# Down projection: the copying and adding transfers of the plain blocks in another order

## The chip, the cores and the metric

The kernel runs on one core of one Trainium2 chip. The metric is device time in microseconds (us), the median of three runs. A separate profiled execution gives the trace from which durations are read.

## What is computed

One decoder layer on 512 tokens of width 1024. Two token mixers and a first layer norm come first; the part that matters here is the end, a gated feed-forward net, a residual and a second layer norm:

```
ff = (silu(h @ w_ff_gate) * (h @ w_ff_up)) @ w_ff_down
x  = layer_norm(DN_ALPHA * h + ff, ln2_g, ln2_b)
```

`w_ff_down` has 2816 rows, that is 22 blocks of 128, and 1024 columns.

## The kernel before

Every matrix product is made of three fp32r products: each operand is rounded to a "hi" part, the remainder is a "lo" part, and hi·hi, hi·lo and lo·hi are summed in PSUM. So each weight tile needs two steps before TensorE (PE) can use it: a rounding to hi, and a subtraction that gives lo.

The down projection treats the first 16 row blocks by a seven-product scheme (products 1 to 7 of sums and differences of quarter matrices, instead of eight). The last 6 row blocks are **plain**: six tiles of 128 x 1024, three for the left half of the columns (`("a", 0..2)`) and three for the right half (`("b", 0..2)`). They are used directly.

`dn_jobs` (L1568) is the order in which PE uses weight tiles: four tiles of product 1, four of 2, four of 5, three plain b, four of 6, four of 3, four of 7, three plain a, four of 4. A tile of a numbered product takes 12 matmuls of 512 columns (`use`, L1676), a plain one 24 (`use_plain`, L1707). The tiles live in five **slots** (`whi0` to `whi4` with `wlo0` to `wlo4`). When PE has used a tile, `release_dn` (L1683) hands its slot to the next entry of `dn_prep` (L1569 to L1572). So entry number n of `dn_prep` starts when use number n-5 is over, and a moved entry starts sooner or later by as many uses as it was moved.

How a tile is prepared depends on its kind (`prepare_dn`, L1588):

- A numbered tile: VectorE (DVE) forms the sum or difference in place where the product needs one, ScalarE (ACT) rounds it (`act.copy`, in `two_steps`, L1583), and DVE subtracts. The subtraction is held back and sent when the next `two_steps` is called (`w.flush`).
- A plain tile does not pass through DVE. GpSimd (POOL) issues a transfer from HBM that rounds on the way into `whi` (L1594; the **rounding** transfer, 512 KB). `plain_lo` then lets ACT write -hi into `wlo` (L1577, "negation" below), and POOL issues a second transfer of the same data that adds to it (L1578; the **adding** transfer), which leaves the remainder. The negation must wait for the rounding transfer to land, the adding transfer for the negation, and PE for the adding transfer.

All engines work strictly in the order in which the program lists their instructions. POOL's twelve transfers thus form one list: a rounding transfer that stands behind an adding transfer is not issued before that one, even if its slot is free.

`events` (L1736) says what else happens behind a given use: pieces of the activations being split (`piece`, `split_plain`), accumulators being added into the residual (`take`), further loads on SyncE (SP), and the calls of `plain_lo`. An event runs before the slot of that use is handed on.

Names in rows: `whi3_db0` is slot 3, plain tile b0; `whi1_d53` is slot 1, product 5, tile 3; `pc41` is the activation piece of product 4, half 1; `fph`, `fpl`, `fqh`, `fql` are the split activations for the plain tiles; `dnx`, `dny`, `dnz`, `dnw` are PSUM accumulators; `hr` is the residual; `lnb2` holds the weights of the second norm.

Of the kernel before, what the change touches and what calls it, by code (L numbers as in the profile page):

```python
# [173 lines left out]
def emit(ctx, tc, i, out):  # L174
# [65 lines left out]
    def home(n, name, dt=F32):  # L240
        return gat(n[1:], name, dt) if isinstance(n, str) else big(n, name, dt)
# [96 lines left out]
    def stt(o, a, s1, b, op0, op1, eng=dve):  # L338
        eng.scalar_tensor_tensor(o, a, s1, b, op0=op0, op1=op1)  # L339

    def tt(o, a, b, op, eng=dve):
        eng.tensor_tensor(o, a, b, op=op)  # L342
# [899 lines left out]
    for n in range(4):  # L1242
        ws = w.views[N_GLU + n]
        bs = []
        for e in range(2):
            b = glu(f"gl{n}{e}")
# [113 lines left out]
    def load_dn(z, block, q):  # L1360
        dn[block, q] = z
        sp.dma_start(z, i["w_dq"][block, q])
# [206 lines left out]
    dn_prep = [(m, u) for m, u in dn_jobs]  # L1569
    for e, m, nxt in (("b", 5, 6), ("a", 7, 4)):  # L1570
        at_ = dn_prep.index((m, 2))
        dn_prep[at_ : at_ + 7] = [(e, 0), (m, 2), (m, 3), (e, 1), (nxt, 0), (e, 2), (nxt, 1)]  # L1572
    dops, dslot, pieces = {}, {}, {}
    half = [slice(1024 * e, 1024 * e + 1024) for e in range(2)]

    def add_remainder(hi, lo, src):
        act.mul(lo, hi.bitcast(F32), -1.0)  # L1577
        pool.dma_start(lo, src, accum_op=ALU.add)  # L1578

    def plain_lo(e, p):  # L1580
        add_remainder(*dops[e, p, "flat"], i["w_dp"]["ab".index(e), p])

    def two_steps(src, hi, lo):  # L1583
        act.copy(hi, src)  # L1584
        w.flush()
        w.after = lambda: tt(lo, src, hi.bitcast(F32), ALU.subtract)
# [26 lines left out]
    def ff_half(q, h):  # L1613
        return ffs[q][:, h].rearrange("p f t -> p (f t)")

    def piece_sum(m, e):
        a11, a21, a12, a22 = (ff_half(q, h) for q in (e, e + 2) for h in range(2))
        if m == 5:
            tt(a21, a21, a22, ALU.add)
        elif m == 6:  # L1620
            tt(a11, a21, a11, ALU.subtract)
        elif m == 3:
            tt(a12, a12, a11, ALU.subtract)
        elif m == 7:
            tt(a21, a22, a11, ALU.subtract)

    def piece(m, e, h):
        a11, a21, a12, a22 = (ff_half(q, hh) for q in (e, e + 2) for hh in range(2))
        src = {1: a11, 2: a12, 5: a21, 6: a11, 3: a12, 7: a21, 4: a22}[m]
        z = home(h, f"pc{m}{e}", F32R).rearrange("p (n c) -> p n c", n=2)  # L1630
        hi, lo = z[:, 0], z[:, 1]
        pieces[m, e] = tuple(z.rearrange("p (f t) -> p f t", f=4) for z in (hi, lo))
        if m in (6, 3, 7):
            piece_sum(m, e)
        two_steps(src, hi, lo)
# [3 lines left out]
    def split_plain(q, h):  # L1639
        hs = slice(0, 2) if q == 5 else slice(h, h + 1)  # L1640
        fs = slice(0, 2 if q == 5 else 4)
        hi, lo = (z[:, hs] for z in plain_ff[q])
        two_steps(ffs[q][:, hs, fs], hi, lo)
# [39 lines left out]
    def release_dn(m, u):  # L1683
        w.held.appendleft(dslot.pop((m, u)))
        w.release()
# [31 lines left out]
    def take(key, n, d, alpha, stats=False):  # L1717
        for e in range(2):
            z = hn[2 * n + e][:, halves[d]]
            if alpha:  # L1720
                stt(z, z, ALPHA, acc[key][e], ALU.mult, ALU.add)
            else:
                tt(z, z, acc[key][e], ALU.add)
            if stats:
                dve.bn_stats(bsts[2 * n + e][:, d, :], z)
# [5 lines left out]
    def finish_tile(t):  # L1731
        normalize_shared(hn[t], mvs[t], lnb2)
        for cs in halves:
# [1 line left out]

    events = {(1, 1): lambda: piece(2, 1, 7), (1, 2): lambda: load_pair(3, 0),  # L1736
              (1, 3): lambda: (take("x", 0, 0, True), piece(5, 0, "g1")),
              (2, 0): lambda: load_pair(3, 1), (2, 1): lambda: piece(5, 1, 8), (2, 3): lambda: plain_lo("b", 0),
              (5, 0): lambda: split_plain(4, 0), (5, 1): lambda: split_plain(4, 1), (5, 2): lambda: plain_lo("b", 1),
              (5, 3): lambda: (take("z", 1, 1, True), piece(6, 0, 7)),  # L1740
              ("b", 0): lambda: (plain_lo("b", 2), piece(6, 1, "g1"), split_plain(5, 1)), ("b", 1): lambda: piece(3, 0, 8),
              ("b", 2): lambda: take("w", 1, 1, False),
              (6, 1): lambda: piece(3, 1, 7), (6, 2): lambda: load_pair(1, 0),
              (6, 3): lambda: (take("x", 0, 1, True), piece(7, 0, "g1")),
              (3, 0): lambda: load_pair(1, 1), (3, 1): lambda: piece(7, 1, 8),
              (3, 3): lambda: plain_lo("a", 0),
              (7, 0): lambda: (load_norm2(), piece(4, 0, 7)), (7, 2): lambda: (plain_lo("a", 1), piece(4, 1, "g1")),
              (7, 3): lambda: take("x", 1, 1, False, True), ("a", 0): lambda: plain_lo("a", 2), ("a", 1): lambda: take("z", 0, 1, False, True)}

    def load_pair(block, q):  # L1750
        load_dn(wp.tile([P, 2048], F32, tag="wraw", name=f"dn{block}{q}", bufs=2), block, q)

    def load_norm2():
        late_["lnb2"] = home(3, "lnb2").rearrange("p (e d) -> p e d", e=2)
        sp.dma_start(late_["lnb2"], i["ln2"].unsqueeze(0).broadcast_to([P, 2, D]))

    late_ = {}
    for m, u in dn_jobs[1:-4]:
        (use_plain if isinstance(m, str) else use)(m, u)
        if (m, u) in events:  # L1760
            events[m, u]()
        release_dn(m, u)
    w.flush()
    lnb2 = late_["lnb2"]
    take("y", 0, 0, False, True)
# [10 lines left out]
    z = hn[2][:, halves[0]]  # L1776
# [5 lines left out]
    z = hn[3][:, 0:256]  # L1782
# [10 lines left out]
    z = hn[3][:, cs]  # L1793
# [94 lines left out]
def build(inputs):  # L1888
    import concourse.bacc as bacc

    a = {k: np.asarray(v) for k, v in inputs.items()}
    arrays = {f"in_{k}": np.ascontiguousarray(v) for k, v in {**layout(a), **constants()}.items()}
    nc = bacc.Bacc("TRN2", target_bir_lowering=False, num_devices=1)
    aps = {k[3:]: nc.dram_tensor(k, v.shape, mybir.dt.from_np(v.dtype), kind="ExternalInput").ap()
           for k, v in arrays.items()}
    out = nc.dram_tensor("out_dram", (S, D), F32, kind="ExternalOutput").ap()
    with tile.TileContext(nc) as tc:  # L1897
        with ExitStack() as ctx:
            with tc.manual_schedule():
                emit(ctx, tc, aps, out)  # L1900
    return nc, arrays
# [8 lines left out]
```

## Time and profile before

| | us |
|---|---|
| median of three runs | 832.65 |
| the three runs | 833.4, 832.65, 830.59 |
| the profiled execution | 829.29 |
| its span in the trace | 827.5 |

The span runs from the first to the last instruction of the trace; the remaining 1.8 us of the profiled execution lie around it. PE is the busiest engine, with 98% of the span, DVE follows with 79%, ACT with 49%, POOL with 9%. The granted TensorE clock was 0.995 on average. The down projection lies at about 700 to 818 us; its first plain tile starts on PE at 735.9 us, the last one at 797.7 us. In the rows of a timeline the columns are start, duration, engine, line, operation, and in square brackets the idle time of the engine before it with what ended it.

### The profile page before, as it was taken

How to read it: one execution, taken by the hardware profiler on the slowest of the kernel's cores; microseconds unless marked ns; L12 is line 12 of the kernel's file. 1: busy time of each engine (PE TensorE's matmuls, PEld its weight loads, DVE VectorE, ACT ScalarE, POOL GpSimd, SP SyncE). 2: the span in 40 equal slices, each digit the busy share in tenths (PEclk: the TensorE clock that was granted, in tenths of full speed). 3: DMA queues.
4: the chain of work that ended last, by engine and by line, in shares of the span. 5: the costliest groups of instructions: out<-in, count | busy, mean ns of one | idle time of the engine just before them, and what ended most of it. 6: DMA issues, size and time to landing. Idle time of an engine off the chain costs nothing. (4 is left out here: it accounts for less than half of the span.)

```text
span 827.5 us, 13778 instructions
## 1 busy us (share of the span) xinstructions
PE 810.3 (98%) x5608; PEld 725.9 (88%) x5608; DVE 653.3 (79%) x1043; ACT 403.0 (49%) x597; POOL 76.2 (9%) x94
## 2 busy tenths in 40 slices
PE   9999999999999999999999999999999999999985
PEld 7888888888899989988888899999999999887864
DVE  7976899673878798655886698877777789887976
ACT  6964331155557535774333355455545446554420
POOL 0000001310011332100000420000000000010014
PEclk9999999999999999999999999999999999999998
DMA  9733434746226654661624143332222235664543
GB/s 335 199 103 138 160 139 130 160 121 204 77 85 145 130 101 113 184 244 51 253 78 177 51 170 137 133 123 102 102 103 102 103 104 196 236 156 124 166 89 101
DMA packets 31471, 116.43 MB, mean 141 GB/s; under 512 B 7600, under 2 KB 12464, under 8 KB 21680
## 3 DMA queue, kind: packets, MB, share of 16 engines
q1 hardware_dynamic: 23808, 91.83, 32.1%
q0 software_dynamic: 5968, 22.02, 12.3%
q10 hardware_dynamic: 1632, 1.70, 0.6%
q8 instruction: 44, 0.72, 0.4%
q14 instruction: 19, 0.16, 0.1%
HBM read 99.55 MB, written 9.70 MB: 132 GB/s over the span
## 5 line engine op out<-in xcount | busy, mean ns | idle before, releaser
L202 DVE TENSOR_TENSOR wlo<-raw,whi 128x1024 fp32r<-128x1024 f32 x52 | 63.8, 1231 | 33.0 <-ACT whi L201 32.9
L201 ACT CAST whi<-raw 128x1024 fp32r<-128x1024 f32 x52 | 54.2, 1046 | 42.5 <-PE pq L209 17.5
L1472 ACT CAST whi<-sums 128x1024 fp32r<-128x1024 f32 x40 | 42.0, 1049 | 66.2 <-DVE sums L342 66.2
L1119 ACT CAST whi_q<-rq 128x1024 fp32r<-128x1024 f32 x28 | 29.2, 1050 | 42.1 <-DVE rq L342 42.1
L342 DVE TENSOR_TENSOR wlo<-sums,whi 128x1024 fp32r<-128x1024 f32 x40 | 48.7, 1218 | 0.0
L342 DVE TENSOR_TENSOR wlo_q<-rq,whi_q 128x1024 fp32r<-128x1024 f32 x28 | 34.0, 1221 | 12.9 <-ACT whi_q L1119 12.8
L1672 PE MATMUL dnx<-whi_d,pc 128*128 128x512 f32 (+1 forms) x128 | 38.2, 376 | 0.0
L208 PE MATMUL pg<-x_hi,whi 128*128 128x512 f32 x96 | 37.6, 392 | 0.0
L209 PE MATMUL pg<-x_lo,whi 128*128 128x512 f32 x96 | 37.4, 389 | 0.0
L210 PE MATMUL pg<-x_hi,wlo 128*128 128x512 f32 x96 | 37.4, 389 | 0.0
L840 ACT ACTIVATE un<-un,st 128x256 f32<-128x256 f32 (+1 forms) x64 | 30.8, 482 | 13.4 <-DVE st L838 13.4
L765 POOL DMA_DIRECT2D kq<-qz x32 | 25.2, 1316 | 108.6 <-PE s L827 47.7
L955 ACT ACTIVATE gt<-pg,bgate 128x512 f32<-128x512 f32 x12 | 8.3, 690 | 42.5 <-PE pg L210 42.5
L1672 PEld LDWEIGHTS dnx<-whi_d,pc 128*128 128x128 f32 x128 | 23.6, 188 | 4.4
L1584 ACT CAST whi_d<-dn 128x1024 fp32r<-128x1024 f32 x16 | 16.8, 1051 | 19.6 <-DVE dn L342 13.1
L208 PE MATMUL pv<-whi,x_hi 128*128 128x512 f32 x64 | 25.4, 397 | 0.0
L209 PE MATMUL pv<-wlo,x_hi 128*128 128x512 f32 x64 | 25.0, 390 | 0.0
L210 PE MATMUL pv<-whi,x_lo 128*128 128x512 f32 x64 | 24.9, 390 | 0.0
L342 DVE TENSOR_TENSOR wlo<-ra,whi 128x1024 fp32r<-128x1024 f32 x20 | 24.4, 1218 | 0.4 <-ACT whi L1472 0.4
L1672 PE MATMUL dnx<-wlo_d,pc 128*128 128x512 f32 (+1 forms) x64 | 24.1, 376 | 0.0
L1594 POOL DMA_DIRECT2D whi_db<-in_w_dp x3 | 2.0, 680 | 238.6 <-PE dny L1672 237.6
L1148 PE MATMUL qx<-x23h,whi_q 128*128 128x256 f32 x80 | 23.2, 290 | 0.7 <-ACT qsnap L1181 0.7
(800 smaller groups left out, 2937.4 us busy)
## 6 DMA issues: line engine op xcount, KB each, us to landing
raw<-in_w_in SPq DMA_DIRECT2D x16, 1024.0 KB, 5.0
ra<-in_w_gu SPq DMA_DIRECT2D x10, 1024.0 KB, 4.7
rb<-in_w_gu SPq DMA_DIRECT2D x10, 1024.0 KB, 4.8
rq<-in_w_quad SPq DMA_DIRECT2D x16, 512.0 KB, 4.2
dn<-in_w_dq SPq DMA_DIRECT2D x8, 1024.0 KB, 4.9
kq<-qz POOLq DMA_DIRECT2D x32, 128.0 KB, 5.7
raw<-in_w_br SPq DMA_DIRECT2D x4, 1024.0 KB, 4.7
raw<-in_w_out SPq DMA_DIRECT2D x4, 1024.0 KB, 4.7
```

What stands on the lines that cost most here:

```text
L201: act.copy(hi, src)
L202: dve.tensor_tensor(lo, src, hi.bitcast(F32), op=ALU.subtract)
L208: pe.matmul(dst, a[0], b[0], start=first, stop=False)
L209: pe.matmul(dst, a[0], b[1], start=False, stop=False)
L210: pe.matmul(dst, a[1], b[0], start=False, stop=last)
L342: eng.tensor_tensor(o, a, b, op=op)
L765: pool.dma_start(dst[32 * q : 32 * q + 32], z[32 * (q ^ 1) : 32 * (q ^ 1) + 32], accum_op=ALU.add)
L840: act.activation(pt, pt, AF.Exp, bias=mneg, scale=-1.0, accum_out=zsum)
L1119: act.copy(hi, src)
L1148: pe.matmul(d[:, 256 * e : 256 * e + 256], p_[:, e, k, :], q_[:, k, :], start=(first and e == k == m == 0), stop=(k == 3 and m == 2), skip ...
L1472: act.copy(hi, src)
L1672: pe.matmul(acc[key][0 if key == "v" else e][:, cs], p_, q_[:, cs], start=(key, e) not in begun, stop=(m == 2), skip_group_check=True)
```

## The change

Two things change, both in the order in which instructions are listed; no instruction is added or taken away, and no matmul changes its place on PE.

First, in `dn_prep` the rounding transfers of b1, b2, a1 and a2 each move forward past one numbered tile: b1 past `(5, 3)`, b2 past `(6, 0)`, a1 past `(7, 3)`, a2 past `(4, 0)`. In turn each of these four numbered tiles starts one use later. The plain tiles a0 and b0 keep their places.

Second, the calls of `plain_lo` leave `events`. The first two of each group run right after the slot of a use has been handed on (`plain_at`), the third one just before the events of a use (`plain_first`). With that, the negations and adding transfers take other places among ACT's and POOL's instructions. The event of `("b", 0)` also lists `split_plain(5, 1)` ahead of `piece(6, 1)` now.

```diff
-        dn_prep[at_ : at_ + 7] = [(e, 0), (m, 2), (m, 3), (e, 1), (nxt, 0), (e, 2), (nxt, 1)]
+        dn_prep[at_ : at_ + 7] = [(e, 0), (m, 2), (e, 1), (m, 3), (e, 2), (nxt, 0), (nxt, 1)]
...
-              (2, 0): lambda: load_pair(3, 1), (2, 1): lambda: piece(5, 1, 8), (2, 3): lambda: plain_lo("b", 0),
-              (5, 0): lambda: split_plain(4, 0), (5, 1): lambda: split_plain(4, 1), (5, 2): lambda: plain_lo("b", 1),
+              (2, 0): lambda: load_pair(3, 1), (2, 1): lambda: piece(5, 1, 8),
+              (5, 0): lambda: split_plain(4, 0), (5, 1): lambda: split_plain(4, 1),
...
-              ("b", 0): lambda: (plain_lo("b", 2), piece(6, 1, "g1"), split_plain(5, 1)), ("b", 1): lambda: piece(3, 0, 8),
+              ("b", 0): lambda: (split_plain(5, 1), piece(6, 1, "g1")), ("b", 1): lambda: piece(3, 0, 8),
...
-              (3, 3): lambda: plain_lo("a", 0),
-              (7, 0): lambda: (load_norm2(), piece(4, 0, 7)), (7, 2): lambda: (plain_lo("a", 1), piece(4, 1, "g1")),
-              (7, 3): lambda: take("x", 1, 1, False, True), ("a", 0): lambda: plain_lo("a", 2), ("a", 1): lambda: take("z", 0, 1, False, True)}
+              (7, 0): lambda: (load_norm2(), piece(4, 0, 7)), (7, 2): lambda: piece(4, 1, "g1"),
+              (7, 3): lambda: take("x", 1, 1, False, True), ("a", 1): lambda: take("z", 0, 1, False, True)}
+    plain_at = {(2, 3): ("b", 0), (5, 1): ("b", 1), (3, 3): ("a", 0), (7, 1): ("a", 1)}
+    plain_first = {(5, 3): ("b", 2), (7, 3): ("a", 2)}
...
     for m, u in dn_jobs[1:-4]:
         (use_plain if isinstance(m, str) else use)(m, u)
+        if (m, u) in plain_first:
+            plain_lo(*plain_first[m, u])
         if (m, u) in events:
             events[m, u]()
         release_dn(m, u)
+        if (m, u) in plain_at:
+            plain_lo(*plain_at[m, u])
```

Where the entries of `dn_prep` start, counted in uses (the use whose end frees the slot):

| rounding transfer of | before | now |
|---|---|---|
| b0 | end of (2, 1) | the same |
| b1 | end of (5, 0) | end of (2, 3) |
| b2 | end of (5, 2) | end of (5, 1) |
| a0 | end of (3, 1) | the same |
| a1 | end of (7, 0) | end of (3, 3) |
| a2 | end of (7, 2) | end of (7, 1) |

On POOL, the transfers of the plain tiles a stand like this before:

```order
L1594 DMA whi2_da0_7585<-in_w_dp 128x1024
L1578 DMA wlo2_da0_7586<-in_w_dp 128x1024
L1594 DMA whi1_da1_7641<-in_w_dp 128x1024
L1578 DMA wlo1_da1_7642<-in_w_dp 128x1024
L1594 DMA whi0_da2_7678<-in_w_dp 128x1024
L1578 DMA wlo0_da2_7679<-in_w_dp 128x1024
```

and like this now:

```order
L1594 DMA whi4_da0_7585<-in_w_dp 128x1024
L1594 DMA whi3_da1_7617<-in_w_dp 128x1024
L1578 DMA wlo4_da0_7586<-in_w_dp 128x1024
L1594 DMA whi2_da2_7656<-in_w_dp 128x1024
L1578 DMA wlo3_da1_7618<-in_w_dp 128x1024
L1578 DMA wlo2_da2_7657<-in_w_dp 128x1024
```

The rounding transfer of a1 now stands ahead of the adding transfer of a0, and that of a2 ahead of the adding transfer of a1. The six transfers of b move in the same way.

On ACT, from the third tile of product 7 to the rounding of the last tile of product 4, before:

```order
L1584 CAST whi0_d72_7600<-dn21_7145 128x1024
L1577 ACTIVATE wlo2_da0_7586<-whi2_da0_7585 128x1024
L1584 CAST whi3_d73_7619<-dn21_7145 128x1024
L1584 CAST pc40_7638<-ff2_5860 128x1024
L1584 CAST whi4_d40_7656<-dn10_7521 128x1024
L1577 ACTIVATE wlo1_da1_7642<-whi1_da1_7641 128x1024
L1584 CAST pc41_7675<-ff3_6295 128x1024
L1584 CAST whi3_d41_7697<-dn10_7521 128x1024
L1577 ACTIVATE wlo0_da2_7679<-whi0_da2_7678 128x1024
L1584 CAST whi2_d42_7728<-dn11_7562 128x1024
L1584 CAST whi1_d43_7761<-dn11_7562 128x1024
```

and now:

```order
L1584 CAST whi1_d72_7600<-dn21_7145 128x1024
L1577 ACTIVATE wlo4_da0_7586<-whi4_da0_7585 128x1024
L1584 CAST pc40_7636<-ff2_5860 128x1024
L1584 CAST whi0_d73_7639<-dn21_7145 128x1024
L1577 ACTIVATE wlo3_da1_7618<-whi3_da1_7617 128x1024
L1584 CAST pc41_7673<-ff3_6295 128x1024
L1584 CAST whi1_d40_7676<-dn10_7521 128x1024
L1577 ACTIVATE wlo2_da2_7657<-whi2_da2_7656 128x1024
L1584 CAST whi0_d41_7699<-dn10_7521 128x1024
L1584 CAST whi4_d42_7728<-dn11_7562 128x1024
L1584 CAST whi3_d43_7761<-dn11_7562 128x1024
```

The negations of a1 and a2 each moved up by one rounding of a product-4 tile, and the rounding of (7, 3) went behind that of `pc40`.

## The prediction

> **What bounds the kernel now.** I read the page first, then the waits of PE, then PE's timeline around the waits, then the lists that feed those waits. The page:
>
> ```profile
> PE 810.3 (98%) x5608; PEld 725.9 (88%) x5608; DVE 653.3 (79%) x1043; ACT 403.0 (49%) x597; POOL 76.2 (9%) x94
> ```
>
> PE is busy in 98% of the span, so what PE waits for can set the time. In the down projection (690 to 828 us), the waits of PE are only these two:
>
> ```profile
> PE dny L1672 <- DMA wlo_da<-in_w_dp: 3.0, 1, 3.0
> PE dnw L1672 <- DMA wlo_db<-in_w_dp: 1.2, 1, 1.2
> ```
>
> Both are for adding transfers of plain tiles. PE's timeline shows where: the second matmul of a tile, the first that reads `wlo`, comes late in b2, a1 and a2 (columns: start, duration, then the idle time).
>
> ```profile
> 746.78 0.39 PE L1672 MATMUL dnw<-whi_db,fqh 128*128 128x512 f32 x1
> 748.38 0.50 PE L1672 MATMUL dnw<-wlo_db,fqh 128*128 128x512 f32 x1 [1.21 <-DMA wlo_db<-in_w_dp]
> 748.72 0.39 PE L1672 MATMUL dnw<-whi_db,fql 128*128 128x512 f32 x1
> ...
> 791.92 0.39 PE L1672 MATMUL dny<-whi_da,fph 128*128 128x512 f32 x1
> 792.34 0.50 PE L1672 MATMUL dny<-wlo_da,fph 128*128 128x512 f32 x1
> 792.68 0.39 PE L1672 MATMUL dny<-whi_da,fpl 128*128 128x512 f32 x1
> ...
> 797.70 0.39 PE L1672 MATMUL dny<-whi_da,fqh 128*128 128x512 f32 x1
> 801.14 0.51 PE L1672 MATMUL dny<-wlo_da,fqh 128*128 128x512 f32 x1 [3.05 <-DMA wlo_da<-in_w_dp]
> 801.49 0.39 PE L1672 MATMUL dny<-whi_da,fql 128*128 128x512 f32 x1
> ...
> 806.38 0.39 PE L1672 MATMUL dnx<-whi_da,fql 128*128 128x512 f32 x1
> ```
>
> The undisturbed step between starts is (806.38 - 801.49) / 21 = 0.233 us in tiles b2 and a2. From the first to the third matmul should take 0.47 us. It takes 1.94 us in b2, so 1.47 are lost; 3.79 us in a2, so 3.32 are lost; and 0.76 us in a1, so 0.3 are lost. Together 5.1 us. This is more than the 4.2 us of the waits view, which leaves out the short one in a1 and what the matmul after a stall is longer (0.50 against 0.39 us).
>
> Why the transfers are late stands in POOL's timeline:
>
> ```profile
> 726.31 0.91 POOL L1578 DMA_DIRECT2D wlo_db<-in_w_dp  x1 [5.65 <-DVE dn L342]
> 728.20 0.56 POOL L1594 DMA_DIRECT2D whi_db<-in_w_dp  x1 [0.98 <-PE dnz L1672]
> 734.56 0.87 POOL L1578 DMA_DIRECT2D wlo_db<-in_w_dp  x1 [5.81 <-ACT wlo_db L1577]
> 735.12 0.86 POOL L1594 DMA_DIRECT2D whi_db<-in_w_dp  x1
> ...
> 778.30 0.87 POOL L1578 DMA_DIRECT2D wlo_da<-in_w_dp  x1 [7.12 <-ACT wlo_da L1577]
> 778.88 0.84 POOL L1594 DMA_DIRECT2D whi_da<-in_w_dp  x1
> 786.95 0.86 POOL L1578 DMA_DIRECT2D wlo_da<-in_w_dp  x1 [7.22 <-DVE bstb L1725]
> 787.51 0.85 POOL L1594 DMA_DIRECT2D whi_da<-in_w_dp  x1
> 795.56 0.87 POOL L1578 DMA_DIRECT2D wlo_da<-in_w_dp  x1 [7.20 <-ACT wlo_da L1577]
> ```
>
> The rounding transfers of b2 (735.12) and a2 (787.51) go out right behind an adding transfer, that of the tile before. Their slots were free sooner. A numbered tile is 12 steps of 0.23 us, about 2.73 us; a1 starts on PE at 791.92, a0 24 steps sooner at 786.48, and (7, 2) ends 2.73 us before that, at 783.75. Its last matmul is out of PE about 0.4 us after its start, so the slot of a2 is free at about 783.9. The transfer goes out 3.6 us later. The same sum for b2: b2 starts at 746.78, b0 two plain tiles sooner at 735.9, (5, 2) ends at 733.2, the slot is free at 733.4, 1.7 us before the issue. That a free slot is otherwise taken at once shows in b1: (5, 0) ends at 727.8, and the transfer goes out at 728.20.
>
> **The change, step by step.** The time from a rounding transfer to a ready tile comes from these rows (issues with sizes and the median time to landing, then one negation):
>
> ```profile
> whi_db<-in_w_dp POOLq DMA_DIRECT2D x3, 512.0 KB, 5.0
> wlo_db<-in_w_dp POOLq DMA_DIRECT2D x3, 512.0 KB, 5.6
> whi_da<-in_w_dp POOLq DMA_DIRECT2D x3, 512.0 KB, 6.7
> wlo_da<-in_w_dp POOLq DMA_DIRECT2D x3, 512.0 KB, 5.4
> ```
> ```profile
> 794.20 1.06 ACT L1577 ACTIVATE wlo_da<-whi_da 128x1024 fp32r<-128x1024 f32 x1 [3.81 <-DMA whi_da<-in_w_dp]
> ```
>
> I take 6.7 us for every rounding transfer, the greater median; 1.06 for the negation; 0.3 from its end to the issue (795.26 to 795.56); 5.6 for the adding transfer. Together 13.7 us. All times below are on the clock of the trace before, as though nothing ahead had moved.
>
> *a2.* Its slot is now that of (7, 1), free 2.73 us before that of (7, 2), at about 781.3, and POOL waits there for nothing else: the adding transfer of a1 stands behind it. Ready at 781.3 + 13.7 = 795.0. Without the stall in a1, PE wants it at 797.4 + 0.2 = 797.6. So the 3.32 us go, with 2.6 us to spare.
>
> *b2.* Slot of (5, 1), free at 730.7; ready at 744.4; wanted at 747.0. The 1.47 us go, with 2.6 to spare.
>
> *a1 and b1.* Both start one use sooner. a1: slot of (3, 3), free at about 775.8 instead of 778.5, ready at 789.5, wanted at 792.15; the 0.3 us go. Its adding transfer stands on POOL behind the rounding of a2, but that is issued at 781.3, and the negation of a1 ends only at 775.8 + 6.7 + 1.1 = 783.6, so nothing is held up. b1 is the same with 725.2 and 738.9, wanted at 741.5.
>
> *a0 and b0.* Their rounding transfers stay; the adding ones now stand on POOL behind the rounding of a1 and b1. Those are issued at 775.8 and 725.2, ahead of the 778.30 and 726.31 at which the adding ones went out. Cost zero on POOL. In the DMA queue, though, they now have a copy ahead of them (below).
>
> *The numbered tiles that start later.* (6, 0) and (4, 0) are used four and more uses after their preparation, with the plain tiles between; the loss of one use is covered. (5, 3) and (7, 3) are prepared two uses before they are wanted. On DVE, the subtraction for (7, 3) is the second of these two:
>
> ```profile
> 778.02 2.50 DVE L342 TENSOR_TENSOR wlo_d<-dn,whi_d 128x1024 fp32r<-128x1024 f32 x2
> ...
> 799.02 1.22 DVE L342 TENSOR_TENSOR wlo_d<-dn,whi_d 128x1024 fp32r<-128x1024 f32 x1 [1.50 <-ACT whi_d L1584]
> 802.62 0.69 DVE L342 TENSOR_TENSOR hr<-hr,dny 128x512 f32<-128x512 f32 x1 [2.37 <-PE dny L1672]
> ...
> 804.74 0.69 DVE L1725 BATCH_NORM_STATS2 bstb<-hr 128x6 f32<-128x512 f32 x1
> 806.81 0.42 DVE L339 SCALAR_TENSOR_TENSOR hr<-hr,dnx 128x256 f32<-128x256 f32 x1 [1.38 <-PE dnx L1672]
> ```
>
> Before, the two stood from 778.02 to 780.52, and the difference for (7, 3) ahead of both. Now the subtraction for (7, 2) comes first, then that difference, then the remainder of `pc40`, then the subtraction for (7, 3): one step of 1.2 us more ahead of it, so it ends at about 781.7. (Its rounding on ACT waits for the slot of (7, 0), 778.5, and for the difference, 779.3, and is over by 780.4.) PE wants it at 786.48 - 2.73 + 0.2 = 784.0. Covered by 2.2 us; each us beyond would be a us of PE. (5, 3) has as much by the same working: its slot is free at 727.9, the rounding takes 1.05 us and DVE is done by about 730, against 733.4.
>
> *The rest.* The negation of b2 now stands on ACT ahead of the rounding of `pc60` and waits for b2's copy, until 730.7 + 6.7 + 1.1 = 738.5; `split_plain(5, 1)` and `piece(6, 1)` change places. Both pieces belong to product 6, which starts only behind b2, at 753; cost zero, and us for us only beyond some 10 us.
>
> *What is late next.* At the end DVE takes over. The last `wlo_d` (799.02) waits for the rounding behind a1, so it moves only by a1's 0.3 us and ends at 799.9. Four steps on `dny` follow, which took from 802.62 to 805.43, 2.8 us; so they end at 802.7. The step on `dnx` (806.81) waits for the end of a2, which moves up by 0.3 + 3.3 us to about 803.2. DVE arrives 0.5 us before it. It had 1.38 us of idle time there before. So a2's gain gets through, but with little to spare; I count 0 to 0.5 us as lost, and take 0.1 since the working says zero. Behind that step everything moves as one piece.
>
> Sum: 1.47 + 0.3 + 3.32 - 0.1 = 5.0 us. The profiled execution would go from 829.29 to 824.3. It lies 3.4 us below the median of the runs shown, 832.65; the same 5.0 us taken off the median gives **827.6 us**.
>
> *A price that the trace shows only from one side.* Where two transfers of 512 KB overlap, the one issued second paid: the rounding of a2 at 787.51, 0.56 us behind an adding one, landed after 6.7 us, while the adding one ahead of it took 5.4. An adding transfer close behind a rounding one does not occur before. Its bounds: nothing added, or the 6.7 - 3.7 = 3.0 us that a rounding transfer paid in second place (3.7 being the quickest landing of a `whi_da`):
>
> ```profile
> DMA to landing us min/median/max: 3.7/6.7/6.7
> ```
>
> At 3.0 us more for each, a0 would be ready at 778.3 + 8.5 = 786.8, against 786.7; b1 and a1 at 741.9 and 792.5, 0.4 us late each; b2 and a2 at 747.4 and 798.0, 0.4 late each: 1.7 us of stalls in all. I take nothing added, because the adding transfers of b2 and a2 have no copy close ahead, and those of the others come 1 us or more behind theirs, further than the 0.56 us of that row.
>
> The Trainium skill, page "DMA: Bandwidth & Descriptors", section "Two DMAs through the same engine are not ordered", says that descriptors within one queue of an engine start in order but overlap; it speaks against this change, since adding transfers now start behind copies that they used to precede. By its section "Anatomy of one DMA — SWDGE (gpsimd) path", moving 512 KB takes 1.2 us beside a fixed 2.0; an estimate from that page is that a copy close ahead adds 1.2 us at most, which every tile's margin here holds, so the sum by the page stays at 5.0. The trace shows a larger price, 3.0 us, and the range uses that.
>
> **Rivals.**
>
> *Part of the gain (0.17).* The second-place price holds in full, or the load of `lnb2`, which waits for the remainder of (7, 3) to free its buffer and so falls into a2's copy, slows that copy by as much. Gain 5.0 - 1.7 = 3.3 us: 829.3. For it: 6.7 against 3.7 us. Against: the margins of 2.6 us.
>
> *DVE takes the place (0.11).* DVE is nearly full ahead of the end (length, then the busy time of PE, PEld, DVE, ACT and POOL, the granted clock, the DMA share and GB/s):
>
> ```profile
> 786.40:797.60 11.20, 11.16 (x50) 8.92 (x49) 11.02 (x13) 4.24 (x5) 2.28 (x3) 1.00 0.50 111
> ```
>
> DVE is busy for 11.02 us of 11.2. If the new order there costs it 3 us, a2's gain is gone: 2.0 us remain, 830.6, no change that can be told. Against: the order only swaps two steps of 1.2 us, `pc41` and the tile (4, 0).
>
> *Slower (0.04).* ACT's list holds. The negation of a1 now stands ahead of `pc41` and the roundings for product 4, and waits there for a1's copy. If that copy, in flight with a0's adding transfer and the `lnb2` load, takes L us, a1 is ready at 775.8 + L + 7.0, wanted at 792.15: from L = 9.3 on, PE pays us for us. To eat the 5.0 us and lose 2.5 more takes L = 16.8, giving 835.2. The longest landing seen is 6.7.
>
> *The forecast (0.68):* the stalls go, 827.6.
>
> **Range and chances.** About 0.3%, 2.5 us, is what a measurement of this kernel can tell from no change. The forecast and the partial gain lie beyond it: faster 0.85. The DVE case: same 0.11. Slower 0.04. The runs shown spread from 830.59 to 833.4, so the low end is 830.59 - 5.1 = 825.5. The high end is the DVE case, 830.6.
>
> **What would show it.** Right: no wait of PE for `wlo` above 0.2 us, the last plain tile 24 steps after the one before, whi_da rounding transfers on POOL without an adding one ahead of each. Wrong: a wait of PE on `wlo_d` in (5, 3) or (7, 3); a `wlo_da` landing after more than 8 us; DVE's step on `dnx` late without a wait for PE; or the waits gone and the span not shorter.

## The result and the profile after

| | before | after |
|---|---|---|
| median of the runs compared | 832.28 us (4 runs) | 825.08 us (4 runs) |
| lowest and highest run | 830.59, 833.4 | 824.76, 825.21 |
| the profiled execution | 829.29 us | 825.21 us |
| its span | 827.5 us | 823.4 us |

The ratio is 0.9915, with a 95% interval from 0.9897 to 0.9932. The kernel became faster by 7.2 us (5.7 to 8.6 by the interval). The forecast was 827.6 us, from 825.5 to 830.6: the direction is right, the gain is 2.2 us larger than the 5.0 forecast, and the median lies 0.4 us below the range. Two more things stand in the table. The runs of the kernel after lie within 0.45 us of each other, those before within 2.8 us. And the two profiled executions differ by only 4.1 us.

The page of the kernel after, busy times first, then the shares of the chain that ended last:

```profile
PE 810.5 (98%) x5608; PEld 726.7 (88%) x5608; DVE 653.4 (79%) x1043; ACT 402.7 (49%) x597; POOL 76.3 (9%) x94
...
PE 92%; DVE 3%; DMA 1%; ACT 1%; POOL 1%; issue 1%; DVEq 0%; SPq 0%; ACTq 0%
```

PE is busy for as long as before, 810.5 against 810.3 us. What became shorter is the time in which it stands. The waits of PE over the whole span (total, times, longest); these are the three longest:

```profile
PE warm_b L286 <- DVE warm L282: 1.1, 1, 1.1
PE qx L1148 <- ACT qsnap L1181: 0.7, 1, 0.7
PE s L827 <- DMA kq<-qz: 0.7, 1, 0.7
```

None of them is in the down projection; both waits for plain tiles are gone. PE's timeline at the start of the last plain tile, a2, confirms it:

```profile
796.95 0.39 PE L1672 MATMUL dny<-whi_da,fqh 128*128 128x512 f32 x1
797.18 0.40 PE L1672 MATMUL dny<-wlo_da,fqh 128*128 128x512 f32 x1
797.42 0.39 PE L1672 MATMUL dny<-whi_da,fql 128*128 128x512 f32 x1
```

The second matmul, the first that reads `wlo`, now comes 0.23 us after the first, as everywhere else. POOL's timeline shows the new order of the transfers (start, duration, line, target, idle time before):

```profile
726.53 0.55 POOL L1594 DMA_DIRECT2D whi_db<-in_w_dp  x1 [4.83 <-PE dny L1672]
727.36 0.90 POOL L1578 DMA_DIRECT2D wlo_db<-in_w_dp  x1 [0.28 <-DVE wlo_d L342]
731.96 0.56 POOL L1594 DMA_DIRECT2D whi_db<-in_w_dp  x1 [3.69 <-PE dnz L1672]
732.51 0.91 POOL L1578 DMA_DIRECT2D wlo_db<-in_w_dp  x1
737.97 0.86 POOL L1578 DMA_DIRECT2D wlo_db<-in_w_dp  x1 [4.55 <-DVE hr L339]
...
775.64 0.56 POOL L1594 DMA_DIRECT2D whi_da<-in_w_dp  x1 [4.87 <-DVE dn L342]
777.88 0.88 POOL L1578 DMA_DIRECT2D wlo_da<-in_w_dp  x1 [1.68 <-ACT wlo_da L1577]
781.08 0.56 POOL L1594 DMA_DIRECT2D whi_da<-in_w_dp  x1 [2.31 <-PE dnx L1672]
781.62 0.91 POOL L1578 DMA_DIRECT2D wlo_da<-in_w_dp  x1
788.29 0.87 POOL L1578 DMA_DIRECT2D wlo_da<-in_w_dp  x1 [5.75 <-ACT wlo_da L1577]
```

The rounding transfers of b2 (731.96) and a2 (781.08) now wait for a matmul, that is for their slot, and for no transfer ahead of them. The last adding transfers go out at 737.97 and 788.29; before, that of a2 went out at 795.56. From issue to landing the tiles a took, whi first, then wlo (each over its three transfers):

```profile
DMA to landing us min/median/max: 3.7/3.8/5.8
...
DMA to landing us min/median/max: 5.6/5.7/8.9
```

The slowest rounding transfer is that of a2 (781.08), the slowest adding one that of a1, 0.55 us behind it. The adding transfer of a2 took 5.7 us, so its tile was ready at 788.29 + 5.7 = 794.0, 3.2 us before PE wanted it at 797.18. At the end, DVE's last steps:

```profile
798.27 1.23 DVE L342 TENSOR_TENSOR wlo_d<-dn,whi_d 128x1024 fp32r<-128x1024 f32 x1 [1.17 <-ACT whi_d L1584]
...
801.45 0.69 DVE L1725 BATCH_NORM_STATS2 bstb<-hr 128x6 f32<-128x512 f32 x1
802.74 0.42 DVE L339 SCALAR_TENSOR_TENSOR hr<-hr,dnx 128x256 f32<-128x256 f32 x1 [0.60 <-PE dnx L1672]
```

DVE still waits for PE ahead of the step on `dnx`, now for 0.60 us (1.38 before). PE is the last to arrive there, so all of a2's gain got through.

### The profile page after: what moved, and what is told of

It is laid out like the page before. It is cut to its first block, busy times and chain, and to the rows that moved or that the text cites. A ratio compares the mean times of both kernels' runs of the same rounds, so it can differ in the third digit from the quotient of the medians.

```text
span 823.4 us, 13781 instructions
## 1 busy us (share of the span) xinstructions
PE 810.5 (98%) x5608; PEld 726.7 (88%) x5608; DVE 653.4 (79%) x1043; ACT 402.7 (49%) x597; POOL 76.3 (9%) x94
## 4 chain that ended last, share of the span: by engine, by line
PE 92%; DVE 3%; DMA 1%; ACT 1%; POOL 1%; issue 1%; DVEq 0%; SPq 0%; ACTq 0%
PE qx L1148 5%; PE dnx L1672 5%; PE dnz L1672 4%; PE pg L208 3%; PE pg L209 3%; PE pg L210 3%; PE pv L208 3%; PE qz L1148 2%; PE pv L209 2%; PE pv L210 2%; PE pu L607 2%; PE dny L1672 2%; PE qy L1148 2%; PE wo L210 2%; PE wo L209 2%; PE b L210 2%
```

## The experiments

The question was where 7.2 us came from when the trace of before held 5.1 us of waits. From the first trace below on, my theory had two parts: the waits go as the prediction worked out; and in most executions, though not in the profiled one, TensorE's clock drops behind the wait in a2, which goes too. The rivals were that the waits are longer in other executions, that the earlier slots alone make the gain, that the order on POOL alone makes it, and that ACT's list matters. Ratios are against the kernel before on the same chip.

**The kernel before again (e1).** No edit.

> The kernel before, unchanged, for a second trace. Theory 1 (the lost time at b2, a1 and a2 differs from execution to execution, and the one profiled execution of before, 829.29 us, caught little of it): what PE loses at these three places is over 5.1 us where the span is over 827.5 us, and the span less this loss stays at 822.4 us within 0.7 us, near the 823.0 to 823.4 us of the changed kernel. Theory 2 (the loss is 5.1 us each time, and the further 2.2 us by which the measured gain, 7.2 us, exceeds the predicted 5.0 lie elsewhere in the kernel): the loss is 5.1 us within 0.3, and a longer span is longer ahead of the down projection or behind it.

Measured: 832.02 us, ratio 1.0014 (0.9999 to 1.0029); the profiled execution took 831.58 us, 2.3 more than the first one. PE's timeline in a2:

```profile
799.35 0.39 PE L1672 MATMUL dny<-whi_da,fqh 128*128 128x512 f32 x1
801.96 0.80 PE L1672 MATMUL dny<-wlo_da,fqh 128*128 128x512 f32 x1 [2.21 <-DMA wlo_da<-in_w_dp]
802.55 0.63 PE L1672 MATMUL dny<-whi_da,fql 128*128 128x512 f32 x1
802.98 0.63 PE L1672 MATMUL dny<-whi_da,fqh 128*128 128x512 f32 x1
...
805.42 0.39 PE L1672 MATMUL dny<-whi_da,fqh 128*128 128x512 f32 x1
```

The wait is shorter than in the first trace (2.21 against 3.05 us), but behind it the step from one matmul to the next is 0.43 us instead of 0.23, until about 805.2. The windows view shows why (length, busy time of PE, PEld, DVE, ACT and POOL, granted clock, DMA share, GB/s), here of this execution:

```profile
802.00:804.00 2.00, 2.00 (x5) 1.62 (x6) 0.00 (x0) 0.00 (x0) 0.00 (x0) 0.50 0.00 0
```

and of the execution that the prediction read, at the same place behind the wait:

```profile
801.10:803.00 1.90, 1.86 (x8) 1.54 (x9) 0.38 (x1) 0.00 (x0) 0.00 (x0) 1.00 0.00 0
```

The granted clock is 0.50 for 3.4 us. In 3.4 us PE makes 3.4 / 0.43 = 8 steps that would take 8 x 0.233 = 1.9 us at full speed, so 1.5 us are lost. The three waits come to 1.5 in b2, 1.2 in a1 and 2.4 in a2, together 5.1. Neither theory on record above had this: the waits are as long as in the first trace, as theory 2 says, but the longer span comes from the matmuls behind a2, which neither names.

**The kernel before, three more times (e12, e13, e14).** No edit; one execution each.

> The kernel before, unchanged, one more trace. Waits alone would explain the missing 2.2 us if what PE loses between the first and third matmul of b1, b2, a1 and a2 came to about 7.3 us with no step at half clock. The clock explains it if the waits come to 5 to 6 us and the rest is matmuls at half speed. In both cases the span less the whole loss should be 822.4 to 823.4 us.

> The kernel before, unchanged, one more trace, read in the same way: waits of 5 to 6 us and some steps at half clock if the clock makes the difference between executions, waits of 7 us and none if the transfers do.

> The kernel before, unchanged, one more trace, read in the same way, so that four traces beside the first one show how often the clock drops behind a2 and by how much the waits differ.

Measured: 831.71, 831.25 and 830.88 us; waits of 5.6, 5.0 and 4.8 us; in each a stretch of 3.41 us at half clock that costs 1.5. Windows of e12, around the end of a2's wait (PE resumes at 801.98):

```profile
802.00:803.40 1.40, 1.40 (x6) 1.17 (x7) 0.00 (x0) 0.00 (x0) 0.00 (x0) 1.00 0.00 0
803.60:806.80 3.20, 3.20 (x9) 2.53 (x8) 2.13 (x4) 0.00 (x0) 0.00 (x0) 0.50 0.00 0
```

The drop came here only 1.5 us after PE had started again. Over five traces of before the waits are 5.1 us on average, as the prediction had it, and four of the five also lose 1.5 us to the clock. The one that I read was the exception. What is left of the span without waits and without the clock's loss is 822.4 to 823.1 us in these five, and 823.4 in the kernel after: nothing else in the kernel became faster.

**One half alone (e2, e3).** The edit of e2; e3 has `"b"` in its place and the calls for b:

```diff
+        dn_prep[at_ : at_ + 7] = ([(e, 0), (m, 2), (e, 1), (m, 3), (e, 2), (nxt, 0), (nxt, 1)] if e == "a" else
+                                  [(e, 0), (m, 2), (m, 3), (e, 1), (nxt, 0), (e, 2), (nxt, 1)])
...
+    plain_at = {(3, 3): ("a", 0), (7, 1): ("a", 1)}
+    plain_first = {(7, 3): ("a", 2)}
```

> The new order for the three plain tiles a alone, b as before. By the rows of before, b2 keeps its 1.5 us and 3.6 us go: a ratio of 0.9957. Theory 1 with the variable part at a2, where the longest chain of transfers stands ahead of PE: 5 to 6 us go, and the runs lie within 0.5 us of each other as those of the changed kernel do. Theory 1 with the variable part at b2: 3.6 us go and the runs still spread over 2 us or more. Theory 2: 3.6 us, whatever the spread.

> The new order for the three plain tiles b alone, a as before. By the rows of before 1.5 us go, a ratio of 0.998, and a1 and a2 keep 3.6 us. Theory 1 with the variable part at a2: 1.5 us go and the runs spread as those of before. Theory 1 with the variable part at b2: 3 to 4 us go. The two parts together, this one and a alone, should give the 7.2 us of the whole change if nothing couples them.

Measured: a alone 826.34 us, ratio 0.9940 (0.9921 to 0.9958), 5.3 us faster; b alone 829.82 us, ratio 0.9977 (0.9964 to 0.9991), 1.8 us faster. Together 7.1: the halves add up to the whole. In the trace of a alone 1.7 us of b2's wait stay, the clock is 1.00 behind a2, and the runs lie within 0.74 us. In that of b alone a1 and a2 still wait, 4.8 us in all, and the clock is at a half for 6.8 us; 1.0 us of that falls into a2's wait, and the rest costs 2.3. The runs of b alone spread by 4.5 us.

**A longer wait, empty and filled (e7, e8).** Both are the changed kernel with a2's negation and adding transfer listed later, so that PE waits in a2. In e8 PE gets 28 matmuls to do meanwhile, into a bank that nobody reads; neither leaves anything of the kernel's work out.

```diff
-    plain_at = {(2, 3): ("b", 0), (5, 1): ("b", 1), (3, 3): ("a", 0), (7, 1): ("a", 1)}
-    plain_first = {(5, 3): ("b", 2), (7, 3): ("a", 2)}
+    plain_at = {(2, 3): ("b", 0), (5, 1): ("b", 1), (3, 3): ("a", 0), (7, 1): ("a", 1), ("a", 1): ("a", 2)}
+    plain_first = {(5, 3): ("b", 2)}
...
+        if (m, u) == ("a", 2):
+            fill(28)
```

The last two lines are those of e8; `fill(n)` issues n matmuls of 128 x 512 on operands that are ready.

> The changed kernel with one step moved: the negation of a2, and with it its adding transfer, goes behind the rounding of the last tile of product 4, so wlo of a2 lands some 7.8 us after PE wants it. Without any price of the clock (1b): 825.1 + 7.8 = 832.9 us. With it (1a): a stretch at half clock behind the wait, 834 to 836 us.

> The same late transfer as in the long wait, with 28 more matmuls ahead of a2 (some 6.4 us, into a free bank that nobody reads), so that PE works through most of the wait. 1b: the time of the long wait or more, since no transfer is sooner and there is more work. 1a: 832.9 us, 1 to 3 us less than the long wait without the fill, and no granted clock below 1.00 behind a2.

Measured: empty 835.05 us, ratio 1.0053 (1.0033 to 1.0073); filled 832.48 us, ratio 1.0019 (1.0006 to 1.0033). With 28 matmuls more the kernel is 2.6 us faster. Windows behind the wait, empty:

```profile
804.40:810.00 5.60, 5.60 (x13) 4.38 (x14) 1.96 (x3) 0.00 (x0) 0.00 (x0) 0.50 0.00 0
```

and filled:

```profile
804.90:810.50 5.60, 5.55 (x24) 4.50 (x25) 2.75 (x4) 0.00 (x0) 0.00 (x0) 1.00 0.02 4
```

In the same 5.6 us PE starts 13 matmuls in the one and 24 in the other. In the empty one the clock is at a half for 10.24 us; 4.2 us of that fall into the wait, and the rest costs 2.8 us. So the cost of an idle wait on PE is the wait and, behind it, the clock; that is shown here apart from every other part of the change.

**The same for the kernel before, and a short wait (e6, e11).** e6 is the kernel before with `fill(10)` ahead of a2; e11 is the changed kernel with a2's negation moved by one tile only, `("a", 0): ("a", 2)` in `plain_at`.

> The kernel before, with ten more matmuls on PE ahead of a2, into a free bank that nobody reads; at 0.23 us each they last 2.3 us, less than PE waits there. No transfer is moved. Theory 1a (behind the wait at a2 the TensorE clock often runs at half speed for some us, which costs 1 to 2.5 us more than the wait itself, and by how much differs between executions): the fill takes this away though it adds work; no granted clock below 1.00 behind a2, a median near 830, that is 1 to 2 us under the kernel before, and a spread well below its 3 to 5 us. Theory 1b (the spread and the extra loss come from the transfers alone): median and spread of the kernel before, 831.6 us or more.

> The changed kernel with the negation of a2 behind the rounding of the third tile of product 4: wlo of a2 lands some 2.3 us after PE wants it, and no other place of the program waits. If a wait this short never lowers the clock: 827.4 us, and runs within 0.5 us of each other as for the changed kernel. If it does so in some executions, by where it falls: runs from 827.4 up to 829.5, the longer ones with a mean granted clock lower by 0.002 or so (a stretch of 3.4 us at half clock loses 1.7 us and takes 0.002 off the mean over 827 us).

Measured: e6 830.39 us against 830.64, ratio 1.0000 (0.9987 to 1.0012). The mean clock was 0.995 to 0.997 in all its 12 runs. (In every trace the last 5 to 8 us are at half clock; in the kernel after, PE's last matmul ends at 813.9 us and the clock falls at 817.9. So the mean is below 1 in any case. In the 16 traces it is 0.995 to 0.997 where there is no other stretch at half clock, and 0.990 to 0.994 where there is one.) So no run of e6 shows a drop behind a2, but the gain of 1 to 2 us that I expected did not come out of the noise. The filling only takes the place of the wait, of which 0.8 us are left behind it (waits and filling in its trace come to 5.6 us; the waits alone came to 5.1 in the first trace), and 15 of the 29 runs of before on that chip also have a mean clock of 0.995 or more, so there was little to win. As a measure of the clock's share it is inconclusive.

Measured: e11 826.86 us, ratio 0.9949 (0.9932 to 0.9966); PE is idle for 2.11 us in a2, and no run shows a drop (0.996 in all six, whose times spread by 1.9 us). An idle time of 2.21 us did bring one in e1. What decides it is not the length alone.

The traces on record say more. In each of the 16, every change of the clock lies a whole number of times 3.413 us behind the moment at which the clock first rose to full (233 times 3.413 us in e1, 234 times in e12). So each trace can be cut into cells of 3.413 us from that moment on. In the trace that the prediction read, the 3.05 us of idle time in a2 fall into two cells, with 1.29 and 1.76 us (the length less PE's busy time), and the next cell is at full clock:

```profile
795.96:799.38 3.42, 2.13 (x10) 1.43 (x8) 1.92 (x3) 1.28 (x2) 0.46 (x1) 1.00 0.68 95
799.38:802.79 3.41, 1.65 (x7) 1.38 (x8) 1.04 (x2) 0.00 (x0) 0.00 (x0) 1.00 0.30 59
802.79:806.21 3.42, 3.42 (x17) 2.73 (x16) 2.57 (x4) 0.00 (x0) 0.00 (x0) 1.00 0.02 7
```

In e9 (below), one idle time of 2.17 us falls into a single cell, and the next cell is at half clock:

```profile
797.41:800.82 3.41, 1.24 (x6) 0.82 (x5) 0.12 (x1) 0.00 (x0) 0.00 (x0) 1.00 0.90 245
800.82:804.24 3.42, 3.42 (x10) 2.64 (x9) 0.45 (x1) 2.47 (x3) 0.87 (x1) 0.50 0.01 4
```

In the same trace, idle times of 2.33 and 2.21 us that lie across two cells each (0.71 + 1.62 and 0.84 + 1.37) brought no drop. Over the full-clock cells of all 16 traces, the next cell is at half clock wherever PE was idle for 1.93 us or more within the cell, and at full clock wherever it was idle for 1.77 us or less; of three cells in between, those with 1.88 and 1.90 us brought a drop and the one with 1.91 us (e11) didn't. This was read out of the traces afterwards; no run was made to test it.

**The slots alone, the calls alone (e5, e9).** e5 is the kernel before with the new row of `dn_prep` only, e9 the changed kernel with the old row:

```diff
-        dn_prep[at_ : at_ + 7] = [(e, 0), (m, 2), (m, 3), (e, 1), (nxt, 0), (e, 2), (nxt, 1)]
+        dn_prep[at_ : at_ + 7] = [(e, 0), (m, 2), (e, 1), (m, 3), (e, 2), (nxt, 0), (nxt, 1)]
```

> The new order of slots, with the calls for the adding transfers where they were before. The rounding transfers of b2 and a2 then stand ahead of the adding transfers of b1 and a1 anyway, and only the places of the adding transfers of b0, a0 and a2 differ from the changed kernel's. If the moved calls themselves are worth something: slower than the changed kernel by over 0.5 us, with a wait of PE for a wlo. If the slots and the order that follows from them are all: 825.1 us within 0.5 us, and no wait of PE for a wlo.

> The complement of the slots alone: the calls for the adding transfers where the changed kernel has them, the slots handed out as before. On POOL every rounding transfer then again stands behind the adding transfer of the tile before. If each half is worth nothing without the other: a2 keeps its 3.3 us of waiting and the stretch at half clock, at most the 1.5 us of b2 go, so 830 us or more, within 0.3% of the kernel before. If the halves just add up, 0.6 us having been measured for the slots: 6 us or more of gain.

Measured: the slots alone 830.01 us, ratio 0.9991 (0.9978 to 1.0004), no change that can be told; the calls alone 838.13 us, ratio 1.0077 (1.0058 to 1.0096), 6 us slower, which neither of the two outcomes on record expected. Together they bring 7.2 us. That the slots alone make the gain is refuted. ACT's timeline with the slots alone:

```profile
786.20 1.06 ACT L1577 ACTIVATE wlo_da<-whi_da 128x1024 fp32r<-128x1024 f32 x1 [4.50 <-DMA whi_da<-in_w_dp]
787.16 1.03 ACT L1584 CAST pc<-ff 128x1024 fp32r<-128x1024 f32 x1
788.10 1.04 ACT L1584 CAST whi_d<-dn 128x1024 fp32r<-128x1024 f32 x1
793.33 1.05 ACT L1584 CAST whi_d<-dn 128x1024 fp32r<-128x1024 f32 x1 [4.19 <-DVE dn L342]
794.29 1.06 ACT L1577 ACTIVATE wlo_da<-whi_da 128x1024 fp32r<-128x1024 f32 x1
```

The rounding transfer of a1 goes out behind the adding one of a0, at 779.95, and lands after 6.2 us. The negation of a1 stands on ACT ahead of the rounding of `pc41` and waits 4.50 us for it. DVE's timeline shows what hangs on that:

```profile
788.23 1.23 DVE L342 TENSOR_TENSOR pc<-ff,pc 128x1024 fp32r<-128x1024 f32 x1 [4.14 <-ACT pc L1584]
```

DVE stands 4.14 us for `pc41` and everything behind it on its list is late, also the difference for (4, 1), whose rounding on ACT (793.33) stands ahead of the negation of a2. So a2, whose copy went out at 782.60 and landed after 6.4 us, at 789.0, is negated at 794.29; its adding transfer goes out at 795.64, as late as in the kernel before. With the calls alone the same happens twice:

```profile
793.14 1.06 ACT L1577 ACTIVATE wlo_da<-whi_da 128x1024 fp32r<-128x1024 f32 x1 [7.39 <-DMA whi_da<-in_w_dp]
...
801.77 1.06 ACT L1577 ACTIVATE wlo_da<-whi_da 128x1024 fp32r<-128x1024 f32 x1 [6.64 <-DMA whi_da<-in_w_dp]
```

The negations stand high on ACT's list while their copies still go out late, and PE's waits come to 10.0 us. This is the mechanism of the prediction's "slower" rival, ACT's list held by a copy.

**The order on POOL, and b2's negation alone (e4, e10).** e4 is the kernel before, with the adding transfers of b1 and a1 listed behind the rounding of b2 and a2. Its edit also changes ACT's list in one place: the negation of a1 goes behind the rounding of `pc41` (787.81 and 784.28 us in its trace; before, it stood ahead, 785.59 and 786.55). e10 is the changed kernel with the negation of b2 put back behind the rounding of `pc60`:

```diff
+    plain_at = {(5, 2): ("b", 1), (7, 2): ("a", 1)}
...
-    plain_first = {(5, 3): ("b", 2), (7, 3): ("a", 2)}
+    plain_first = {("b", 0): ("b", 2), (7, 3): ("a", 2)}
```

The first line is e4's, the other two are e10's.

> The slots are handed out as before, so no rounding transfer may start a use sooner; only the adding transfers of b1 and a1 are listed behind the rounding transfers of b2 and a2. If the standing behind an adding transfer is the main cause: b2's rounding goes out 1.7 us sooner and a2's 3.6 us sooner, so the 1.5 us at b2 and the 3.3 us at a2 go almost whole, and a1's 0.3 us stay or grow to some 1 us, since its adding transfer now has a copy ahead: 4 to 5 us of gain by the rows of before. If the slots are the main cause: 1 us or less.

> The changed kernel with one step put back: the negation of b2 stands on ACT behind the roundings of pc60 and of the second tile of product 6 again, which wait for DVE. POOL's list is that of the changed kernel, and the rounding transfer of b2 goes out 3 to 4 us sooner than before. If the place on ACT alone can hold b2: the negation starts near 742 us however soon the copy lands, PE loses some 1.5 us at b2, 826.6 us. If POOL's list was the limit, as the prediction had it: no loss, 825.1 us.

Measured: e4 827.02 us, ratio 0.9945 (0.9926 to 0.9964); e10 826.74 us, ratio 0.9944 (0.9924 to 0.9965), 1.7 us behind the changed kernel by the medians and 2.4 by the ratios. The waits of PE in e4:

```profile
PE dnw L1672 <- DMA wlo_db<-in_w_dp: 1.8, 2, 1.4
PE dny L1672 <- DMA wlo_da<-in_w_dp: 0.8, 1, 0.8
```

The wait in a2 is gone; the one left for `wlo_da` is a1's. The edit brings 4.6 of the 7.2 us (831.6 to 827.02, against the kernel before on its chip). That is the gain that was expected, but not for the reason expected: b2's wait stays, and the half clock behind a2 goes with a2's wait. The rounding transfer of a2 goes out at 785.73, as soon as PE has released its slot, so POOL's list did hold it before, as the prediction said. It was not a2's only limit. In e5 that transfer also goes out ahead of a1's adding one (782.60 and 787.56), and a2 still waits 2.6 us, because `pc41` stands behind a1's negation on ACT; in e4 it doesn't. b2 still waits in e4, and ACT's timeline says why:

```profile
738.52 1.05 ACT L1584 CAST pc<-ff 128x1024 fp32r<-128x1024 f32 x1 [3.83 <-DVE ff L342]
740.87 1.06 ACT L1584 CAST whi_d<-rb 128x1024 fp32r<-128x1024 f32 x1 [1.29 <-DVE rb L342]
741.83 1.06 ACT L1577 ACTIVATE wlo_db<-whi_db 128x1024 fp32r<-128x1024 f32 x1
```

b2's transfer went out at 734.21 and had landed after 4.1 us, at 738.3, but its negation stands behind two roundings that wait for DVE. In e10, where the slot is the early one too, the picture is the same:

```profile
740.50 1.06 ACT L1584 CAST whi_d<-rb 128x1024 fp32r<-128x1024 f32 x1 [1.29 <-DVE rb L342]
741.46 1.06 ACT L1577 ACTIVATE wlo_db<-whi_db 128x1024 fp32r<-128x1024 f32 x1
```

and b2's wait of 2.2 us is the only one left. In the kernel before, ACT's list had the same order:

```profile
740.30 1.05 ACT L1584 CAST whi_d<-rb 128x1024 fp32r<-128x1024 f32 x1 [1.29 <-DVE rb L342]
741.42 1.06 ACT L1577 ACTIVATE wlo_db<-whi_db 128x1024 fp32r<-128x1024 f32 x1
```

There b2's copy, out at 735.12, landed after 6.3 us, at 741.4, when ACT was through with that rounding too. For b2 there were two limits at once, and the change had to lift both.

## Why the prediction was right, and where it was wrong

**Right: which waits go, and how much they are.** b2, a1 and a2 wait no more, and five traces of before put these waits at 5.1 us on average, the prediction's own sum. DVE at the end took nothing of it (0.60 us to spare, 0.5 forecast). The subtraction for (7, 3) ended at 781.4, which is 780.4 on the clock of the trace before (781.7 forecast), and neither (5, 3) nor (7, 3) makes PE wait.

**Wrong: "the same 5.0 us taken off the median".** This is the step that failed. The sum was made against one execution that lay 3.4 us under the median, and the gap was carried over as though it had nothing to do with the change. Part of it had: in four of five traces of before TensorE runs at half clock behind a2's wait for 3.41 us, which costs 1.5 us, and without the wait there is no such drop in the kernel after. 5.1 + 1.5 = 6.6 us, inside the interval of 5.7 to 8.6. The runs say the same: among 70 of the kernel before, the 23 with a mean clock of 0.995 or more have a median of 830.09 us, the 47 below it one of 831.96. The first is 5.0 us above the kernel after, the size of the forecast. The profiled execution had the longest idle time of the five in a2, but it lay across two cells of 3.413 us; in the other four, 1.93 to 2.58 us of it lay in one. The remaining 0.6 us of 7.2 can't be told from the differences between chips, on which the median of before lay from 830.64 to 832.28 us. The size in e1 and e7 and the filled wait of e8 show the clock; how large its share is in the timed runs is worked out, not measured alone, since e6 was inconclusive.

The profiles look as though the forecast had been too high, 4.1 us instead of 5.0. The kernel after reached its down projection later: its first matmul there on `dnx` starts at 701.4 us, before at 700.3. The 1.0 us lies ahead of everything that was changed.

The range failed with this step. Its low end took the lowest run shown and subtracted the waits, so it allowed for no second loss that goes with them. The spread of before's runs, 2.8 us, was a hint that something differs from run to run, and the profile showed an execution without the drop. It was no proof: the runs of e6, none of which shows a drop, spread by 3.7 us, so the clock is not all that varies. The Trainium skill, page "TensorE: Matmul & The Clock Gate", section "Part 1: The HAM clock gate", has the rule that was missed: a window of 4096 cycles, about 3.4 us, that runs freely and lowers the clock to a half when it has been idle. The stretches here, 3.41, 6.83 and 10.24 us, are one, two and three such windows. By these traces a window need not be idle throughout: 1.93 us of 3.41 were enough in e12. The Trainium skill, in the section "Why this matters for your kernels" of the same page, advises against idle gaps of more than about 3 us; that is too mild by these traces, since 2.17 us were enough in e9 and 2.21 us in e1.

**Right, but too simple: POOL's list.** The prediction named only POOL's list as the reason why a2 and b2 are late. POOL's list held both, but ACT's list was a second limit. For b2 the prediction counted the move of the negation on ACT as "cost zero"; e10 shows that the move is worth about 2 us (1.7 by the medians, a wait of 2.2 us in its trace): without it b2 waits as before. For a2 it is e5 that shows it.

**Right by a margin: the second-place price.** The prediction took nothing for an adding transfer behind a rounding one, because they would come 1 us or more apart. They came 0.55 us apart twice (732.51 and 781.62): a1's copy took 3.7 us where I had taken 6.7, so its adding transfer was ready when a2's rounding went out. And they paid: 7.6 us for b1 instead of 5.6, and 8.9 us for a1, that is 3.3 more, a little over the bound of 3.0 and over the 8 us that the prediction had named as a sign of being wrong. How much of a1's is the copy's doing isn't shown, since the load of `lnb2` was in flight too; b1 had no such load. The copy ahead paid as well, 5.8 against 3.7 in a2. b0's adding transfer came only 0.83 us behind a copy, not 1 us; it took 5.6 us here, but 7.3 to 7.8 in the traces of e3, e7, e8, e10 and e11. No wait came of it, since a1 landed at 781.62 + 8.9 = 790.5 and PE wanted it at 791.7. So the spare of 1.2 us in a1 is the smallest that the change leaves, not a2's 3.2.

**The rival "slower".** Its place and its cause were right and it did not decide: in the changed kernel the copy of a1 lands before ACT comes to its negation. With the old slots it does decide (e9, 6 us slower), and with the new slots and the old calls it takes a2's gain back (e5). The change works because its two parts are made together.

## What to carry to other kernels

Where the runs of a kernel spread by more than those of its neighbours, look at several traces before you subtract a saving from the median: the profiled one may lack a loss that goes with the wait you remove. A wait of 2 to 3 us on TensorE can cost half as much again behind it. And when a transfer is late, follow both lists that it hangs on, the one that issues it and the one that prepares it: lifting one limit of two brought nothing (the slots alone) or harm (the calls alone).

## What the runs showed of the hardware

- The half clock comes in pieces of 3.41 us (3.41 six times, 6.83 once, 10.24 once, the end of the program left aside) and can set in after PE has resumed, by 1.5 us in e12. Its changes lie on a grid of 3.413 us in every trace. An idle time of 3.05 us across two cells of the grid brought none, one of 2.17 us within a cell did (e9); over 16 traces the edge lies between 1.77 and 1.93 us of idle time within one cell. No run was made to test this.
- Of two transfers of 512 KB that POOL issued 0.55 us apart, an adding one in second place took 7.6 us (b1) and 8.9 us (a1, with a load of 1 MB issued 0.15 us before it) in the kernel after, against 5.6 to 5.7 us for the other adding ones there. The copy ahead took 4.6 and 5.8 us, against 3.7 to 3.8 for the other copies. The other way round, in the first trace of before, the adding one ahead kept its 5.4 to 5.6 us and the copy behind paid all (6.3 and 6.7 us). A median over three transfers hid this; the least and the greatest showed it.
